# Ten tiles in one 51-token buffer: a weighted pair sum with rooms of 13, 13, 13 and 12 tokens, a GpSimd share in one tile, and the last three stores on SyncE

## The chip, the core and the metric

The kernel runs on one core of a Trainium2 chip. The core has a memory of 128 partitions (SBUF), and engines that work side by side: VectorE (DVE in the profile), ScalarE (ACT), GpSimd (POOL) and SyncE (SP), which here only issues transfers. Data come from and go to the main memory (HBM) by DMA: an engine's queue issues a transfer, and 16 DMA engines carry it out. The metric is the time of one execution in microseconds of the device (us); lower is better. The profile's span runs from the first to the last instruction and is a little shorter than this time.

## What is computed

```python
batch, seq, hidden, n_experts, k = 16, 1024, 512, 8, 2
# expert_outputs: (batch, seq, k, hidden) float32;  combine_weights: (batch, seq, k) float32
weights = combine_weights[..., np.newaxis]
out = np.sum(expert_outputs * weights, axis=2).astype(np.float32)
```

For each of 16,384 tokens, two vectors of 512 numbers are multiplied by a weight each and added. 64 MiB are read and 32 MiB are written.

## The kernel before

Each partition holds 128 tokens ("rows" in what follows): a row is one token in each of the 128 partitions, 4 KB per partition to read and 2 KB to write. The first 120 rows are laid out so that partition p has 120 neighbouring tokens, 480 KB; the last 8 rows are a second block of the same kind. The tiles are 12 rows, ten times, and then one of 8. Four buffers take turns, so a load of tile g waits until the store of tile g - 4 has landed.

```python
    per = n // P                     # 128 rows
    J, LAST = 12, 8
    main = per - LAST                # 120
    def rows(x):
        a = x[0 : P * main, :].rearrange("(p t) f -> p t f", p=P)
        b = x[P * main : n, :].rearrange("(p t) f -> p t f", p=P)
        return lambda t, c: a[:, t : t + c, :] if t < main else b[:, t - main : t - main + c, :]
    # ... (types; eo, cw and o are inputs and output seen through rows)
    last = main // J                 # 10
    ipool = ctx.enter_context(tc.tile_pool(name="in", bufs=4))
    # ... (weights wt: two small loads from ScalarE's queue; one activation to load its table)
    for g in range(last + 1):
        et = ipool.tile([P, J, k * h], dt)
        ot = et.rearrange("p j f -> p (j f)")[:, 0 : J * h].rearrange("p (j f) -> p j f", f=h)
        t0, c = g * J, J if g < last else LAST
        for a, m in ((0, 2), (2, c - 2)) if g == 0 else ((0, c),):
            nc.sync.dma_start(out=et[:, a : a + m], in_=eo(t0 + a, m), max_dma_last_dim=...)   # loads
        if g < last - 1:
            # wb: the tile's weights, each broadcast over 512 numbers; ek: et as 2 c vectors
            nc.vector.tensor_tensor(out=ek, in0=ek, in1=wb, op=mult)
            nc.vector.tensor_tensor(out=ot, in0=et[:, :, 0:h], in1=et[:, :, h : 2 * h], op=add)
            nc.scalar.dma_start(out=o(t0, c), in_=ot)                    # stores, ScalarE's queue
            continue
        for i in range(c):           # the last two tiles
            t = t0 + i
            nc.scalar.activation(out=et[:, i, 0:h], in_=et[:, i, 0:h], func=copy, scale=wt[:, 2*t : 2*t+1])
            if g == last:            # last tile: row by row, behind ScalarE
                nc.vector.scalar_tensor_tensor(out=ot[:, i, :], in0=et[:, i, h : 2 * h],
                    scalar=wt[:, 2*t+1 : 2*t+2], in1=et[:, i, 0:h], op0=mult, op1=add)
        if g < last:                 # last but one: VectorE multiplies the second vectors, then adds
            # w1: second weight of each row, broadcast; x1 = et[:, :, h : 2 * h]
            nc.vector.tensor_tensor(out=x1, in0=x1, in1=w1.to_broadcast([P, c, h]), op=mult)
            nc.vector.tensor_tensor(out=ot, in0=et[:, :, 0:h], in1=x1, op=add)
        nc.sync.dma_start(out=o(t0, c), in_=ot[:, 0:c])                  # last two stores, SyncE's queue
```

The sums are written over the tile's own first half, and stored from there. The order in which a queue issues is set by the scheduler that turns this text into a program, not by the text alone.

Of the kernel before, what the change touches and what calls it, by code (L numbers as in the profile page):

```python
# [1 line left out]

# [4 lines left out]


@with_exitstack
def kernel(  # L10
    ctx: ExitStack,
    tc: tile.TileContext,
    expert_outputs: bass.AP,
    combine_weights: bass.AP,
    out: bass.AP,
):

    nc = tc.nc  # L20
    b, s, k, h = expert_outputs.shape
    assert k == 2
    n = b * s
    P = nc.NUM_PARTITIONS
    per = n // P
    assert per * P == n
    J, LAST = 12, 8
    main = per - LAST
    assert main % J == 0
    eo = expert_outputs.rearrange("b s k h -> (b s) (k h)")  # L30
    cw = combine_weights.rearrange("b s k -> (b s) k")
    o = out.rearrange("b s h -> (b s) h")
# [7 lines that stand above are left out]
    eo, cw, o = rows(eo), rows(cw), rows(o)  # L40

    dt = mybir.dt.float32
    mult = mybir.AluOpType.mult
    add = mybir.AluOpType.add
    copy = mybir.ActivationFunctionType.Copy

    last = main // J

    wpool = ctx.enter_context(tc.tile_pool(name="w", bufs=1))
    ipool = ctx.enter_context(tc.tile_pool(name="in", bufs=4))  # L50

    wt = wpool.tile([P, per * k], dt)

    for t, c in ((0, main), (main, LAST)):
        nc.scalar.dma_start(
            out=wt[:, k * t : k * (t + c)].rearrange("p (t k) -> p t k", k=k), in_=cw(t, c)
        )

    warm = wpool.tile([P, 1], dt)
    nc.scalar.activation(out=warm, in_=nc.const_aps.tensor(1.0, (P, 1), dt), func=copy)  # L60

    for g in range(last + 1):
        et = ipool.tile([P, J, k * h], dt)

        ot = et.rearrange("p j f -> p (j f)")[:, 0 : J * h].rearrange("p (j f) -> p j f", f=h)
        t0, c = g * J, J if g < last else LAST

        for a, m in ((0, 2), (2, c - 2)) if g == 0 else ((0, c),):
            nc.sync.dma_start(  # L69
                out=et[:, a : a + m],  # L70
                in_=eo(t0 + a, m),
                max_dma_last_dim=k * h * 4 if g + a == 0 else None,
            )
        if g < last - 1:

            wb = wt[:, g * J * k : (g + 1) * J * k].unsqueeze(2).to_broadcast([P, J * k, h])
            ek = et.rearrange("p j (k h) -> p (j k) h", k=k)
            nc.vector.tensor_tensor(out=ek, in0=ek, in1=wb, op=mult)  # L78
            nc.vector.tensor_tensor(out=ot, in0=et[:, :, 0:h], in1=et[:, :, h : 2 * h], op=add)  # L79
            nc.scalar.dma_start(out=o(t0, c), in_=ot)  # L80
            continue


        for i in range(c):
            t = t0 + i
            nc.scalar.activation(  # L86
                out=et[:, i, 0:h], in_=et[:, i, 0:h], func=copy, scale=wt[:, 2 * t : 2 * t + 1]
            )
            if g == last:
                nc.vector.scalar_tensor_tensor(  # L90
                    out=ot[:, i, :],
                    in0=et[:, i, h : 2 * h],
                    scalar=wt[:, 2 * t + 1 : 2 * t + 2],
                    in1=et[:, i, 0:h],
                    op0=mult,
                    op1=add,
                )
        if g < last:
            w1 = wt.rearrange("p (t k) -> p t k", k=k)[:, t0 : t0 + c, 1:2]
            x1 = et[:, :, h : 2 * h]  # L100
            nc.vector.tensor_tensor(out=x1, in0=x1, in1=w1.to_broadcast([P, c, h]), op=mult)  # L101
            nc.vector.tensor_tensor(out=ot, in0=et[:, :, 0:h], in1=x1, op=add)  # L102
        nc.sync.dma_start(out=o(t0, c), in_=ot[:, 0:c])


# [1 line left out]
_INS = ['expert_outputs', 'combine_weights']  # L107
_OUTS = [((16, 1024, 512), 'float32')]


# [23 lines left out]
```

## Time and profile before

| | |
|---|---|
| time, median of 3 runs | 239.04 us (238.97 to 239.12) |
| span in the profile | 237.3 us |
| VectorE busy | 193.9 us (82%), 28 instructions |
| ScalarE busy | 14.0 us (6%), 22 instructions |
| GpSimd busy | 0.2 us (four fills at the start) |
| HBM read / written | 67.24 MB / 33.55 MB, 425 GB/s over the span |
| load of 12 rows, issue to landing, median | 29.9 us |
| store of 12 rows from ScalarE's queue, issue to landing, median | 32.7 us |

In the profile's groups a line reads: line of the kernel, engine, operation, output and inputs with their shapes, count; then total busy us and mean ns of one; then the engine's idle time before these instructions and what ended it. Lines 78 and 79 are the multiply and the add of an ordinary tile, 86 the ScalarE multiply of the last two tiles, 90 the row-by-row operation of the last tile, 101 and 102 the multiply and add of the last but one. Line 69 issues loads, 80 the stores from ScalarE, 103 those from SyncE. A "q" after an engine's name is its queue of DMA issues.

### The profile page before, as it was taken

The numbers are of one execution on the slowest core, as the hardware profiler recorded it, in microseconds if no ns is written. First come the engines' busy times: TensorE is split into PE (matmuls) and PEld (weight loads), VectorE is DVE, ScalarE is ACT, GpSimd is POOL, SyncE is SP. The second block draws the span as 40 slices with busy tenths as digits, with TensorE's granted clock in tenths as the row PEclk, the third lists the DMA queues.
The fourth block names the chain that finished last, engine by engine and source line by source line (L and its number), as shares of the span: only waits on it lengthen the run. The fifth ranks groups of instructions, "written<-read, shape, count | busy, mean of one in ns | idle before, by whom it ended". The sixth has DMA issues, their size and how long they took to land.

```text
span 237.3 us, 154 instructions
## 1 busy us (share of the span) xinstructions
DVE 193.9 (82%) x28; ACT 14.0 (6%) x22; POOL 0.2 (0%) x4
## 2 busy tenths in 40 slices
DVE  0008999999999999999999879969996998785710
ACT  2000000000000000000000000000000000740800
POOL 0000000000000000000000000000000000000000
DMA  8999999989899999999897999999997979999997
GB/s 308 443 456 406 398 431 497 398 356 505 356 439 435 427 464 464 398 398 522 348 522 344 452 427 435 464 464 398 398 522 340 530 336 460 458 403 442 402 438 309
DMA packets 3728, 100.80 MB, mean 425 GB/s; under 512 B 528, under 2 KB 656, under 8 KB 912
## 3 DMA queue, kind: packets, MB, share of 16 engines
q1 hardware_dynamic: 2144, 72.35, 71.1%
q10 hardware_dynamic: 1584, 28.44, 27.9%
HBM read 67.24 MB, written 33.55 MB: 425 GB/s over the span
## 4 chain that ended last, share of the span: by engine, by line
DMA 59%; DVE 33%; ACT 2%; DVEq 0%; ACTq 0%; issue 0%; SPq 0%
DMA et<-in_expert_outputs_dram 30%; DMA out_dram<-et 29%; DVE et L78 22%; DVE et L79 11%; ACT et L86 2%; DVE et L90 1%; DVEq L129 0%; ACTq L129 0%; SPq L69 0%; DVEq L78 0%; ACTq L86 0%
## 5 line engine op out<-in xcount | busy, mean ns | idle before, releaser
L78 DVE TENSOR_TENSOR et<-et,wt 128x12288 f32<-128x12288 f32 x9 | 116.6, 12955 | 25.2 <-DMA et<-in_expert_outputs_dram 25.2
L79 DVE TENSOR_TENSOR et<-et 128x6144 f32<-128x6144 f32 x9 | 59.0, 6558 | 0.3
L86 ACT ACTIVATE et<-et,wt 128x512 f32<-128x512 f32 x20 | 12.5, 707 | 209.2 <-DMA et<-in_expert_outputs_dram 209.2
L90 DVE SCALAR_TENSOR_TENSOR et<-et,wt 128x512 f32<-128x512 f32 x8 | 5.6, 748 | 3.9 <-ACT et L86 3.7
L101 DVE TENSOR_TENSOR et<-et,wt 128x6144 f32<-128x6144 f32 x1 | 6.6, 6559 | 2.3 <-DMA et<-in_expert_outputs_dram 2.3
L102 DVE TENSOR_TENSOR et<-et 128x6144 f32<-128x6144 f32 x1 | 6.6, 6559 | 0.9 <-ACT et L86 0.9
L60 ACT ACT_TABLE_LOAD x1 | 1.3, 1283 | 1.7 <-issue 1.7
L60 ACT ACTIVATE warm<-const-float32-1.0 128x1 f32<-128x1 f32 x1 | 0.2, 202 | 0.0
L118 POOL MEMSET const-bfloat16-1.0<- 128x1 bf16 x1 | 0.1, 102 | 0.0
L118 POOL MEMSET const-uint8-127<- 128x1 uint8 x1 | 0.1, 102 | 0.0
L118 POOL MEMSET const-float32-0.0<- 128x1 f32 x1 | 0.1, 99 | 0.2 <-issue 0.2
L118 POOL MEMSET const-float32-1.0<- 128x1 f32 x1 | 0.1, 99 | 0.0
## 6 DMA issues: line engine op xcount, KB each, us to landing
et<-in_expert_outputs_dram SPq DMA_DIRECT2D x9, 6144.0 KB, 29.9
out_dram<-et ACTq DMA_DIRECT2D x9, 3072.0 KB, 32.7
et<-in_expert_outputs_dram SPq DMA_DIRECT2D x1, 5120.0 KB, 17.3
et<-in_expert_outputs_dram SPq DMA_DIRECT2D x1, 4096.0 KB, 25.1
out_dram<-et SPq DMA_DIRECT2D x1, 3072.0 KB, 14.6
out_dram<-et SPq DMA_DIRECT2D x1, 2048.0 KB, 10.0
et<-in_expert_outputs_dram SPq DMA_DIRECT2D x1, 1024.0 KB, 5.4
wt<-in_combine_weights_dram ACTq DMA_DIRECT2D x1, 120.0 KB, 4.4
```

The source lines that it names most:

```text
L60: nc.scalar.activation(out=warm, in_=nc.const_aps.tensor(1.0, (P, 1), dt), func=copy)
L78: nc.vector.tensor_tensor(out=ek, in0=ek, in1=wb, op=mult)
L79: nc.vector.tensor_tensor(out=ot, in0=et[:, :, 0:h], in1=et[:, :, h : 2 * h], op=add)
L86: nc.scalar.activation(out=et[:, i, 0:h], in_=et[:, i, 0:h], func=copy, scale=wt[:, 2 * t : 2 * t + 1])
L90: nc.vector.scalar_tensor_tensor(out=ot[:, i, :], in0=et[:, i, h : 2 * h], scalar=wt[:, 2 * t + 1 : 2 * t + 2], in1=et[:, i, 0:h], op0=mul ...
L101: nc.vector.tensor_tensor(out=x1, in0=x1, in1=w1.to_broadcast([P, c, h]), op=mult)
L102: nc.vector.tensor_tensor(out=ot, in0=et[:, :, 0:h], in1=x1, op=add)
L118: nc = _bacc.Bacc("TRN2", target_bir_lowering=False, num_devices=1)
```

## The change

The tiles become 13, 13, 13, 12 rows, twice, and then two of 13: ten in all. They lie in four "rooms" of one buffer of 51 rows, where before there were four buffers of 12. The first block is now 115 rows (460 KB per partition), the second 13. Fewer and larger tiles use the SBUF that was left over. In the last tile but one, ScalarE multiplies the first vectors of seven rows and GpSimd those of the other six, while VectorE multiplies the second vectors; for this tile VectorE reads its weights from a copy in PSUM, a separate memory of the core, so that it has one input in SBUF and can run beside GpSimd. The stores of the last three tiles go out from SyncE's queue, behind the last loads, where before it was the last two.

```diff
-    J, LAST = 12, 8
+    rooms = [13, 13, 13, 12]
+    sizes = rooms * 2 + [13, 13]
+    LAST = sizes[-1]
     main = per - LAST
...
-    ipool = ctx.enter_context(tc.tile_pool(name="in", bufs=4))
+    ipool = ctx.enter_context(tc.tile_pool(name="in", bufs=1))
+    ppool = ctx.enter_context(tc.tile_pool(name="pw", bufs=1, space=bass.MemoryType.PSUM))
...
-    for g in range(last + 1):
-        et = ipool.tile([P, J, k * h], dt)
+    pw = ppool.tile([P, sizes[-2] * k], dt)
+    nc.vector.tensor_copy(out=pw, in_=wt[:, k * (main - sizes[-2]) : k * main])
+    room = ipool.tile([P, sum(rooms), k * h], dt)
+    t0 = 0
+    for g, c in enumerate(sizes):
+        at = sum(rooms[: g % len(rooms)])
+        et = room[:, at : at + c]
...
-            nc.scalar.dma_start(out=o(t0, c), in_=ot)
-            continue
-        for i in range(c):
+        else:
+            m = c if g == last else 7
+            for i in range(m):
                 # ScalarE's multiply; in the last tile VectorE's row operation behind it, as before
...
-        if g < last:
-            w1 = wt.rearrange("p (t k) -> p t k", k=k)[:, t0 : t0 + c, 1:2]
+            if g < last:
+                w0 = wt.rearrange("p (t k) -> p t k", k=k)[:, t0 + m : t0 + c, 0:1]
+                w1 = pw.rearrange("p (t k) -> p t k", k=k)[:, :, 1:2]
+                x0, x1 = et[:, m:c, 0:h], et[:, :, h : 2 * h]
+                nc.gpsimd.tensor_tensor(
+                    out=x0, in0=x0, in1=w0.to_broadcast([P, c - m, h]), op=mult
+                )
                 # VectorE's multiply of x1 by w1 and its add, as before
...
-        nc.sync.dma_start(out=o(t0, c), in_=ot[:, 0:c])
+        queue = nc.scalar if g < last - 2 else nc.sync
+        queue.dma_start(out=o(t0, c), in_=ot)
+        t0 += c
```

More of the change, by code (lines that the diff above doesn't have):

```diff
@@ L26 @@
     assert per * P == n
-    J, LAST = 12, 8
+    rooms = [13, 13, 13, 12]
+    sizes = rooms * 2 + [13, 13]
+    assert sum(sizes) == per
+    LAST = sizes[-1]
     main = per - LAST
-    assert main % J == 0
     eo = expert_outputs.rearrange("b s k h -> (b s) (k h)")
@@ L45 @@
     copy = mybir.ActivationFunctionType.Copy
-    last = main // J
+    last = len(sizes) - 1
     wpool = ctx.enter_context(tc.tile_pool(name="w", bufs=1))
-    ipool = ctx.enter_context(tc.tile_pool(name="in", bufs=4))
+    ipool = ctx.enter_context(tc.tile_pool(name="in", bufs=1))
+    ppool = ctx.enter_context(tc.tile_pool(name="pw", bufs=1, space=bass.MemoryType.PSUM))
     wt = wpool.tile([P, per * k], dt)
@@ L60 @@
     nc.scalar.activation(out=warm, in_=nc.const_aps.tensor(1.0, (P, 1), dt), func=copy)
-    for g in range(last + 1):
-        et = ipool.tile([P, J, k * h], dt)
-        ot = et.rearrange("p j f -> p (j f)")[:, 0 : J * h].rearrange("p (j f) -> p j f", f=h)
-        t0, c = g * J, J if g < last else LAST
+    pw = ppool.tile([P, sizes[-2] * k], dt)
[5 more added lines that the diff above has]
+        et = room[:, at : at + c]
+        ek = et.rearrange("p j (k h) -> p (j k) h", k=k)
+        ot = ek[:, 0:c]
         for a, m in ((0, 2), (2, c - 2)) if g == 0 else ((0, c),):
@@ L74 @@
         if g < last - 1:
-            wb = wt[:, g * J * k : (g + 1) * J * k].unsqueeze(2).to_broadcast([P, J * k, h])
-            ek = et.rearrange("p j (k h) -> p (j k) h", k=k)
+            wb = wt[:, t0 * k : (t0 + c) * k].unsqueeze(2).to_broadcast([P, c * k, h])
             nc.vector.tensor_tensor(out=ek, in0=ek, in1=wb, op=mult)
             nc.vector.tensor_tensor(out=ot, in0=et[:, :, 0:h], in1=et[:, :, h : 2 * h], op=add)
-            nc.scalar.dma_start(out=o(t0, c), in_=ot)
-            continue
@@ L84 @@
-        for i in range(c):
[L85 to L96, printed above, removed]
-                )
@@ L98 @@
-        if g < last:
-            w1 = wt.rearrange("p (t k) -> p t k", k=k)[:, t0 : t0 + c, 1:2]
-            x1 = et[:, :, h : 2 * h]
-            nc.vector.tensor_tensor(out=x1, in0=x1, in1=w1.to_broadcast([P, c, h]), op=mult)
-            nc.vector.tensor_tensor(out=ot, in0=et[:, :, 0:h], in1=x1, op=add)
-        nc.sync.dma_start(out=o(t0, c), in_=ot[:, 0:c])
+        else:
+            m = c if g == last else 7
+            for i in range(m):
+                t = t0 + i
+                nc.scalar.activation(
+                    out=et[:, i, 0:h], in_=et[:, i, 0:h], func=copy, scale=wt[:, 2 * t : 2 * t + 1]
+                )
+                if g == last:
+                    nc.vector.scalar_tensor_tensor(
+                        out=ot[:, i, :],
+                        in0=et[:, i, h : 2 * h],
+                        scalar=wt[:, 2 * t + 1 : 2 * t + 2],
+                        in1=et[:, i, 0:h],
+                        op0=mult,
+                        op1=add,
+                    )
[5 more added lines that the diff above has]
+                    out=x0, in0=x0, in1=w0.to_broadcast([P, c - m, h]), op=mult
+                )
+                nc.vector.tensor_tensor(out=x1, in0=x1, in1=w1.to_broadcast([P, c, h]), op=mult)
+                nc.vector.tensor_tensor(out=ot, in0=et[:, :, 0:h], in1=x1, op=add)
```

## The prediction

> **What bounds the kernel now.** I read the page's DMA parts first, because the arithmetic is small against the bytes: 67.24 MB are read and 33.55 MB written. Then I asked for the busy time in stretches, the waits, the groups, and the timeline of the end.
>
> ```profile
> DMA  8999999989899999999897999999997979999997
> ...
> q1 hardware_dynamic: 2144, 72.35, 71.1%
> q10 hardware_dynamic: 1584, 28.44, 27.9%
> ```
>
> The last column is packet time as a share of 16 engines' span. 71.1 + 27.9 = 99.0% of 237.3 us is 234.9 us per DMA engine, so 2.4 us of the span hold no transfer. The stretches show where (columns: stretch, length, busy of VectorE, ScalarE and GpSimd, clock, DMA share, GB/s; a packet counts where it starts):
>
> ```profile
> 0.00:2.00 2.00, 0.00 (x0) 0.26 (x1) 0.20 (x4) 1.00 0.20 31
> 2.00:20.00 18.00, 1.36 (x1) 1.22 (x2) 0.00 (x0) 1.00 1.06 441
> 20.00:60.00 40.00, 39.93 (x5) 0.00 (x0) 0.00 (x0) 1.00 0.99 423
> 60.00:120.00 60.00, 59.90 (x7) 0.00 (x0) 0.00 (x0) 1.00 1.00 433
> 120.00:180.00 60.00, 54.50 (x6) 0.00 (x0) 0.00 (x0) 1.00 1.00 433
> 180.00:220.00 40.00, 32.63 (x4) 7.53 (x13) 0.00 (x0) 1.00 1.00 430
> 220.00:236.00 16.00, 5.57 (x8) 4.94 (x8) 0.00 (x0) 1.00 0.99 424
> 236.00:237.30 1.30, 0.00 (x0) 0.00 (x0) 0.00 (x0) 1.00 0.00 0
> ```
>
> From 2 to 236 us the DMA share is 0.99 to 1.06: the transfers never pause, not even while the last tile is computed. The idle 2.4 us are the start (first packet near 1.8 us) and the final wait. VectorE is at 82% and waits for data:
>
> ```profile
> DVE et L78 <- DMA et<-in_expert_outputs_dram: 25.2, 4, 18.6
> ...
> SPq L69 <- DMA out_dram<-et: 173.8, 7, 45.5
> ```
>
> 18.6 of the 25.2 us are the first load; the other three waits are 2.2 us each, one per tile late in the run. SyncE's 173.8 us are loads waiting for a store to free their buffer; with other transfers always pending, that wait costs nothing. At 433 GB/s a row (one token of each of the 128 partitions) costs 0.524 MB / 433 = 1.21 us to load and 0.605 us to store, 1.815 us together. Twelve rows make 21.8 us, and the late VectorE tiles start at 137.66, 159.43 and 181.13, which is 21.7 us apart. So **the bound is the bytes**, from end to end.
>
> **What the skill says.** "DMA: Bandwidth & Descriptors", section "Where 436 GB/s comes from", gives 16 ports a ceiling of 435.2 GB/s; the 433 here agrees, so nothing is left in the rate. Its section "Queues, rings and completion order" says that SyncE and ScalarE each own a queue on the same 16 engines, consumed in order, and that an engine alternates between queues packet by packet. Here a load's packet is 48 KB and a store's 24 KB, so two busy queues share 2:1; a 6,144 KB load needs 12 x 1.21 = 14.5 us alone and landed after a median 29.9 us, which fits the sharing. "SBUF — State Buffer", section "SBUF: two separate sides", says VectorE with two SBUF inputs and GpSimd lock each other out of a shared port pair; this is why the change puts one tile's weights into PSUM. No run so far shows it. "GPSIMD Engine Reference", section 3.1, has 4,497 ns for a two-input fp32 operation of 2,048 elements; I use it below.
>
> **Part 1: ten tiles instead of eleven.** Bytes stay. One load and one store go. Queue q10 has 1,584 packets for 11 DMAs, so 144 each: 128 of data and 16 of completion, or 8 + 1 per engine. By the packet records a 49,152-byte packet takes 1.815 us and a 24,576-byte one 0.912, so the fixed part is 2 x 0.912 - 1.815 = 0.009 us. Two DMAs x 9 packets x 0.009 = **0.16 us saved**. The first load grows a row, so VectorE begins 1.2 us later, at about 19.8; the second load is already queued behind it, and DMA loses nothing.
>
> **Part 2: VectorE's work.**
>
> ```profile
> L78 DVE TENSOR_TENSOR et<-et,wt 128x12288 f32<-128x12288 f32 x9 | 116.6, 12955 | 25.2 <-DMA et<-in_expert_outputs_dram 25.2
> L79 DVE TENSOR_TENSOR et<-et 128x6144 f32<-128x6144 f32 x9 | 59.0, 6558 | 0.3
> L86 ACT ACTIVATE et<-et,wt 128x512 f32<-128x512 f32 x20 | 12.5, 707 | 209.2 <-DMA et<-in_expert_outputs_dram 209.2
> L90 DVE SCALAR_TENSOR_TENSOR et<-et,wt 128x512 f32<-128x512 f32 x8 | 5.6, 748 | 3.9 <-ACT et L86 3.7
> ```
>
> A row of an ordinary tile costs (12.955 + 6.558) / 12 = 1.626 us. Eight such tiles hold 102 rows: 165.9 us. The last but one costs 13/12 x 6.56 = 7.1 us for the multiply and 7.1 for the add, 14.2. The last took 5.78 us for 8 rows, so 13 take 9.4. The sum is 189.5 against 193.9. A tile of 13 needs 21.1 us of VectorE and 13 x 1.815 = 23.6 of DMA: the bound stays with DMA, and VectorE's 4.4 us are worth nothing. The copy of 26 weights to PSUM falls between their landing (about 5 us) and the first tile.
>
> **Part 3: GpSimd.** Six rows are 3,072 elements; from the skill's figure an estimate of 3,072/2,048 x 4.5 = 6.7 us. ScalarE's seven rows cost 7 x 0.707 = 4.9, VectorE's multiply beside them 7.1. All three end near 7.2 us after the load, against 7.5 now for 12 rows (202.96 to 210.46).
>
> **Part 4: the end.** The last load is now 13 rows instead of 8, with 3.6 us more VectorE work between it and the last store. Is DMA kept busy? Count back from the last byte, at 235.9. Three stores are queued behind the last load on SyncE: 12, 13 and 13 rows, 7.3 + 7.9 + 7.9 = 23.1 us. So the last load's bytes end at 235.9 - 23.1 = 212.8. It lands 0.8 us later; VectorE runs from 214.3 (one ScalarE row first) to 223.7. The last store is needed at 235.9 - 7.9 = 228.0, and reaches the engines 1.1 us after issue (the first load: 0.73 to 1.8), so VectorE may end at 226.8: **3.1 us of slack**. The last store but one is needed at 220.1, so its add must end by 219.0. Its load ends before the last load's 15.7 us, by 197.1; with 0.8 and 7.2 + 7.1 that is 212.2, or 6.8 us of slack. GpSimd could take twice its estimate. So the longer tail is covered, because 7.3 + 7.9 us of stores wait behind the last load. Sum: 239.04 - 0.16 = **238.9 us**.
>
> **Rivals.** (a) *SyncE's order puts a store before the last load.* The source asks for tile 7's store before the loads of tiles 8 and 9, and SyncE waits in order. For: that store comes early in the text. Against: the queue is reordered by when things are ready. Before, tile 9's store also stands ahead of load 10, yet the load went out at 194.8 and the store at 217.0. Load 9 needs tile 5's store landed: VectorE has done six tiles (77 rows) at 19.8 + 77 x 1.626 = 145, and the median store, 32.7 us for 12 rows, is 35.4 for 13, so about 180. The store of tile 7 needs its add: 19.8 + 165.9 = 185.7 and two waits of some 2 us, about 190. That is 10 us of margin instead of 22. If it happened for load 9, that load's end would move 7.3 us later, 4.2 beyond the slack: 243.2 us. For load 8 too, some 10 us more: about 253. I give this 7%.
> (b) *The longer tail shows.* If GpSimd and VectorE blocked each other through the whole tile, 6.7 us would come on top of 14.3; that still fits the 6.8 us. Only past this does each further microsecond count: 240 to 242. About 5%.
> (c) *The transfers get cheaper.* A 460 KB pitch instead of 480 KB could suit memory better. The 20 to 60 us stretch ran at 423 GB/s: 40 x 10/433 = 0.9 us below the later rate. Some of that might come back: 238.0. Nothing in the profile offers more.
> (d) *VectorE becomes the bound.* At 21.1 against 23.6 us a tile this has no support.
>
> **Range and chances.** The 234.9 us of packet time stay under any arrangement, so 2% faster (234.3) would need a faster transfer rate: 1%. Slower by 2% (243.8) needs rival (a) in its worse form: 4%. Range 238.2 to 240.0; below it stands (c) in full, above it (a) and (b).
>
> **What would show it.** Right: DMA share near 1.00 in every stretch up to 1.5 us from the end; VectorE waits of about 2.5 us for late loads; SyncE issuing both last loads ahead of the three stores; last landing near 213.6; VectorE done near 224. Wrong: a stretch after 200 us with a DMA share under 0.9, a store between the last loads on SyncE, an add of the last tile but one ending after 219, or a steady rate that is not 433 GB/s.

## The result, and the profile after

The kernel after takes 239.74 us (median of 6 runs, 239.40 to 240.45) against 239.04 for the kernel before: a ratio of 1.0031, with a 95% interval of 1.0016 to 1.0045. Beside the last experiments it was timed again: 240.08 us (12 runs, 239.93 to 240.49), ratio 1.0032 (1.0016 to 1.0048). By these ratios the change costs about 0.75 us, a small loss but clear of noise, where a gain of 0.16 was predicted. The ratio is not simply the quotient of the two medians: the runs of the kernel before spread to 240.9 us, as the table below shows, and the medians alone differ by 0.70 and 1.04 us.

The DMA queues of the kernel after (queue and kind; packets, MB, share of 16 engines' span):

```profile
q1 hardware_dynamic: 2144, 77.07, 75.3%
q10 hardware_dynamic: 1296, 23.72, 23.1%
```

98.4% of 238.7 us is 234.9 us of packet time per DMA engine, as before, although 288 packets are gone. The same stretches, with the last one longer by the growth of the span (columns as in the prediction; the GpSimd column is the third count):

```profile
20.00:60.00 40.00, 39.93 (x4) 0.00 (x0) 0.00 (x0) 1.00 1.00 421
60.00:120.00 60.00, 59.90 (x7) 0.00 (x0) 0.00 (x0) 1.00 1.00 433
120.00:180.00 60.00, 54.39 (x6) 0.00 (x0) 0.00 (x0) 1.00 1.00 434
180.00:220.00 40.00, 29.51 (x11) 9.53 (x16) 5.32 (x1) 1.00 1.00 431
220.00:236.00 16.00, 4.72 (x8) 2.95 (x5) 0.00 (x0) 1.00 0.99 426
236.00:238.70 2.70, 0.00 (x0) 0.00 (x0) 0.00 (x0) 1.00 0.05 20
```

The transfers still never pause, and the steady rate is still 433. The 421 GB/s from 20 to 60 us, for 423 before, is no clear sign: in e12, the same kernel once more, that stretch has 423 again. What differs is the end. After 236 us, where the kernel before started no packet, a few still start, and so they do in e12:

```profile
236.00:238.30 2.30, 0.00 (x0) 0.00 (x0) 0.00 (x0) 1.00 0.06 23
```

A share of 0.05 over all 16 engines is one or two engines that finish late.

The end, in order of time (start, duration, engine, line, operation):

```profile
184.16 0.33 SPq L80 DMA_DIRECT2D room<-in_expert_outputs_dram  x1
...
191.22 33.85 SPq L118 DMA_DIRECT2D out_dram<-room  x3
195.16 4.40 ACT L96 ACTIVATE room<-room,wt 128x512 f32<-128x512 f32 x7 [191.92 <-DMA room<-in_expert_outputs_dram]
195.16 7.09 DVE L115 TENSOR_TENSOR room<-room,pw 128x6656 f32<-128x6656 f32 x1 [3.96 <-DMA room<-in_expert_outputs_dram]
195.36 5.32 POOL L112 TENSOR_TENSOR room<-room,wt 128x3072 f32<-128x3072 f32 x1 [194.92 <-DMA room<-in_expert_outputs_dram]
202.38 7.09 DVE L116 TENSOR_TENSOR room<-room 128x6656 f32<-128x6656 f32 x1
214.87 8.07 ACT L96 ACTIVATE room<-room,wt 128x512 f32<-128x512 f32 x13 [15.31 <-DMA room<-in_expert_outputs_dram]
215.63 9.09 DVE L100 SCALAR_TENSOR_TENSOR room<-room,wt 128x512 f32<-128x512 f32 x13 [6.16 <-ACT room L96]
```

SyncE issued the last load at 184.16, ahead of the three stores. GpSimd ran beside VectorE's multiply, which took 7.09 us, as long as in e3 without GpSimd. VectorE ended at 224.7. So the tail works as described, and the loss must be elsewhere.

**Where the time went.** Dividing the DMA share by the rate, short windows show how long a packet took. Around the first store the kernel before shows

```profile
38.00:40.00 2.00, 2.00 (x2) 0.00 (x0) 0.00 (x0) 1.00 0.93 393
40.00:42.00 2.00, 2.00 (x1) 0.00 (x0) 0.00 (x0) 1.00 1.16 393
```

and the kernel after

```profile
42.00:44.00 2.00, 2.00 (x1) 0.00 (x0) 0.00 (x0) 1.00 0.99 426
44.00:46.00 2.00, 2.00 (x1) 0.00 (x0) 0.00 (x0) 1.00 1.21 426
46.00:48.00 2.00, 2.00 (x1) 0.00 (x0) 0.00 (x0) 1.00 1.54 586
```

In each pair the same bytes start in 2 us, but their packets take 25% (before) and 22% (after) longer in the second window. In the third, 1.54 / 586 is 13% over 0.99 / 426. The records of single packets say it exactly. The first store is issued at 38 us (before) and 41 us (after). Some 3 us later each engine starts a load packet that stands next to its first store packet, and this load takes 0.3 to 0.6 us longer than normal (1.815 us for 48 KB, 1.966 for 52 KB). The records don't name the engine, but each large packet starts where another has just ended, to within a few ns, so that they can be joined into 16 chains. Before, there is about one such packet per engine. After, 14 engines have two, while the other two have one packet each that is 1.19 and 1.44 us too long. Once this turn from loads alone to loads and stores is over, packets take their normal time to the end. The Trainium skill's "DMA: Bandwidth & Descriptors", section "The descriptor swizzle", has each engine serve its own set of partitions in a transfer over all 128. The records agree in number: the 128 packets of the last store of e8 and of e11, which start after a pause, come in eight rounds of 16. So an engine that falls behind stays behind (the trace after is of the longest of its six runs): before, all end by 236.17; after, 14 end by 236.3 and those two at 237.05 and 237.46. In all but one of the profiles made here, the time is the last engine's last byte plus 2.9 to 3.1 us (after 237.46 and 240.45, before 236.17 and 239.08).

### The profile page after: what moved, and what is told of

Its sections match the earlier page's. It is cut to its first block, busy times and chain, and to the rows that moved or that the text cites. A ratio compares the mean times of both kernels' runs of the same rounds, so it can differ in the third digit from the quotient of the medians.

```text
span 238.7 us, 162 instructions
## 1 busy us (share of the span) xinstructions
DVE 188.7 (79%) x32; ACT 14.0 (6%) x22; POOL 5.5 (2%) x5
## 4 chain that ended last, share of the span: by engine, by line
DMA 63%; DVE 28%; ACT 2%; issue 0%; DVEq 0%; ACTq 0%; SPq 0%
DMA room<-in_expert_outputs_dram 35%; DMA out_dram<-room 28%; DVE room L88 18%; DVE room L89 9%; DVE room L100 2%; ACT room L96 2%; DVEq L144 0%; ACTq L144 0%; SPq L80 0%; DVEq L88 0%; ACTq L96 0%
## 5 line engine op out<-in xcount | busy, mean ns | idle before, releaser
L88 DVE TENSOR_TENSOR room<-room,wt 128x13312 f32<-128x13312 f32 (+1 forms) x8 | 110.0, 13756 | 19.8 <-DMA room<-in_expert_outputs_dram 19.8
L89 DVE TENSOR_TENSOR room<-room 128x6656 f32<-128x6656 f32 (+1 forms) x8 | 55.7, 6958 | 0.3
L96 ACT ACTIVATE room<-room,wt 128x512 f32<-128x512 f32 x20 | 12.5, 710 | 207.2 <-DMA room<-in_expert_outputs_dram 207.2
L100 DVE SCALAR_TENSOR_TENSOR room<-room,wt 128x512 f32<-128x512 f32 x13 | 8.9, 748 | 6.4 <-ACT room L96 6.2
L115 DVE TENSOR_TENSOR room<-room,pw 128x6656 f32<-128x6656 f32 x1 | 7.1, 7086 | 4.0 <-DMA room<-in_expert_outputs_dram 4.0
L112 POOL TENSOR_TENSOR room<-room,wt 128x3072 f32<-128x3072 f32 x1 | 5.3, 5320 | 194.9 <-DMA room<-in_expert_outputs_dram 194.9
L116 DVE TENSOR_TENSOR room<-room 128x6656 f32<-128x6656 f32 x1 | 7.1, 7092 | 0.1
```

What stands on the lines that cost most here:

```text
L112: nc.gpsimd.tensor_tensor(out=x0, in0=x0, in1=w0.to_broadcast([P, c - m, h]), op=mult)
```

## The experiments

All were compared with the kernel before on the same chip. "Long packets" is the sum of time over the normal from 35 to 65 us, as a mean per DMA engine, and "last byte" is when the slowest engine ended; both are from the packet records of the one run that was traced.

| run | tiles, first block | median us (range, runs) | ratio (95%) | long packets | last byte |
|---|---|---|---|---|---|
| before | 12, 480 KB | 239.04 to 239.13 in four groups (238.94-240.89) | 1 | 0.60 | 236.17 |
| after | 13, 460 KB | 239.74 (239.40-240.45, 6) | 1.0031 (1.0016-1.0045) | 0.86 | 237.46 |
| e1 | 12, 460 KB, one tile in two pieces | 240.90 (239.41-241.15, 10) | 1.0063 (1.0045-1.0081) | 0.44 | 236.39 |
| e2 | 13, 480 KB | 239.88 (239.49-240.53, 21) | 1.0024 (1.0011-1.0036) | 1.10 | 236.87 |
| e3 | 13, 460 KB | 240.32 (239.99-241.11, 9) | 1.0042 (1.0024-1.0060) | 1.04 | 237.20 |
| e4 | 13, 460 KB | 240.13 (239.61-240.33, 11) | 1.0037 (1.0025-1.0050) | 0.92 | 237.32 |
| e5 | 12, 480 KB | 239.98 (239.07-241.05, 16) | 1.0013 (0.9993-1.0033) | 0.71 | 237.06 |
| e6 | 13, 460 KB | 239.93 (239.59-240.45, 22) | 1.0019 (1.0006-1.0031) | 0.74 | 237.01 |
| e7 | first 12, 460 KB | 261.57 (260.16-262.30, 6) | 1.0921 (1.0884-1.0957) | 0.38 | 257.14 |
| e8 | 13, 460 KB | 244.34 (244.02-246.05, 4) | 1.0223 (1.0185-1.0262) | 1.02 | 240.93 |
| e9 | 13, one queue | 242.46 (242.15-242.57, 4) | 1.0133 (1.0107-1.0160) | 0.74 | 239.44 |
| e10 | 12, one queue | 243.34 (243.08-243.89, 4) | 1.0175 (1.0146-1.0204) | 1.43 | 240.88 |
| e11 | 13, 460 KB | 247.49 (246.98-247.56, 4) | 1.0346 (1.0315-1.0378) | 0.90 | 243.97 |
| e12 | after again | 240.08 (239.93-240.49, 12) | 1.0032 (1.0016-1.0048) | 1.01 | 237.09 |

The spread matters. The kernel before and e5 have runs down to 238.9 and 239.07, and others up to 240.9 and 241.05. No run of any kernel with 13-row tiles was below 239.40.

With two queues the long packets follow the first large store, not the layout: 0.86 to 1.10 us where it has 13 rows (after, e2, e3, e4, e8, e11, e12), 0.38 to 0.74 where it has 12 (before, e1, e5, e6, e7). The second group includes 460 KB layouts (e1, e6, e7), and in e7 loads of 13 rows beside that store. It is one trace of each kernel, and the time does not follow this mean: e1 has few long packets in its trace, and a long time.

The late engines can be followed further. A load packet over 1.1 us too long stands right behind its engine's first store packet, and that engine began to store about 2 us before the rest: two engines in the trace after (44.75 and 45.07, the others from 46.58), three in e4, one in e5 (41.70, the others from 43.37), four in e12. In each of these four traces as many engines end late, 0.5 us or more behind the rest. In e3 five begin early and five end late. In the kernel before all 16 begin within 43.26 to 43.78, and none ends late. So late engines go with a first store that begins in two groups. They need not: in e2 nine begin early and seven later, and the ends are even. What decides it was not tested.

**e1, the layout alone.** From the kernel before:

```diff
-    main = per - LAST
+    main = 115
+    def parts(t, c):
+        return ((t, c),) if t >= main or t + c <= main else ((t, main - t), (main, t + c - main))
# loads and SyncE's stores go over parts(t0, c)
```

> The kernel before (tiles of 12, last 8) with the first block cut to 115 rows, 460 KB per partition; the tile that crosses the boundary is loaded and stored in two pieces, two transfers more (0.16 us). Theory S, layout: the loss comes from DMA engines that are stalled for unequal times when the first stores meet the loads, and the layout in memory sets how unequal: 239.6 to 240.1, some engines over 0.5 us later than the rest at the end, runs spread by over 0.5 us. Theory S, tile size: the same stalls, but set by the 13-row packets: 239.1 to 239.3 with the spread of before. Theory G (GpSimd, PSUM and the rest of the new program cost a fixed time): 239.1 to 239.3.

240.90 us: time is lost without larger tiles, and more than the theory had. The edit also cuts a tile in two pieces, and no run separates that from the layout, so that the layout is the cause is not shown. And the profiled run was one of only two in ten near 239.4, and it has few long packets. So the trace doesn't show what the other eight runs lost; that stays open.

**e2, the large tiles alone.** From the kernel after:

```diff
-    sizes = rooms * 2 + [13, 13]
+    sizes = rooms * 2 + [9, 9, 8]
-            m = c if g == last else 7
+            m = c if g == last else 5
```

> The kernel after, but tiles of 13, 13, 13, 12 twice and then 9, 9, 8, so that the first block has 120 rows and 480 KB per partition as before; GpSimd has four of the nine rows of the last tile but one. As many transfers as before. Layout: 239.0 to 239.2, engines ending together. Tile size: 239.5 to 239.9, stragglers. Fixed cost of GpSimd and PSUM: 239.6 to 239.8.

239.88 us, with the most long packets of the two-queue runs (1.10 us per engine). Time is lost without the new layout. e2 also holds the rest of the change. Against e5 below, which has that rest with 12-row tiles, its median is no longer (239.98), but none of its 21 runs is below 239.49, where seven of e5's 16 are at 239.25 or less: with 13-row tiles the shortest times are gone. Here no engine is far behind: the 16 engines end evenly from 236.2 to 236.9, where those of the kernel before end from 235.7 to 236.2.

**e3, without GpSimd and PSUM.** From the kernel after:

```diff
-            m = c if g == last else 7
+            m = c
-                w1 = pw.rearrange("p (t k) -> p t k", k=k)[:, :, 1:2]
+                w1 = wt.rearrange("p (t k) -> p t k", k=k)[:, t0 : t0 + c, 1:2]
# pw, its copy and the GpSimd multiply are gone
```

> The kernel after without GpSimd and without the weights in PSUM: ScalarE multiplies all 13 rows of the last tile but one. Stalled engines: 239.7, as after, because that tile has slack. Fixed cost of GpSimd and PSUM: 238.9 to 239.1.

240.32 us: no time comes back, so GpSimd and PSUM are not the cost. The add begins 8.1 us after the load's landing instead of 7.2, inside the slack.

**e4, an early write.** From the kernel after:

```diff
     nc.scalar.activation(out=warm, in_=nc.const_aps.tensor(1.0, (P, 1), dt), func=copy)
+    nc.scalar.dma_start(out=o(0, 1)[:, :, 0:1], in_=warm.unsqueeze(2))
```

> The kernel after with one small store at about 3 us: 4 bytes to the first output row of every partition, overwritten later by the first real store. If the stalls at 44 to 48 us are the price of the first write to each partition's stretch of the output, they go or move to about 4 us, and the time is 239.0 to 239.4. If they come from reads and writes meeting, whatever was written before, the long packets at 44 to 48 us stay and the time is 239.7.

240.13 us, and 29 of 30 clearly long load packets (by over 0.1 us) still lie from 44 to 48 us. So an earlier write of 4 bytes to each partition's stretch of the output does not take them away.

**e5, the rest of the change alone.** From the kernel after:

```diff
-    rooms = [13, 13, 13, 12]
-    sizes = rooms * 2 + [13, 13]
+    rooms = [12, 12, 12, 12]
+    sizes = rooms * 2 + [12, 12, 8]
```

> Everything of the change but its sizes: tiles of 12 (last 8) in four rooms of one buffer, 480 KB per partition, GpSimd with five rows of the last tile but one, weights in PSUM, last three stores on SyncE. Theory: the loss lies in DMA engines that stall when the first store begins, more with 13-row packets; then this is the kernel before in time, 239.0 to 239.2, with a mean stall near 40 us of about 0.6 us per engine. Rival: the three stores on one queue or GpSimd cost time at the end; then 239.5 to 239.9, with a pause of the transfers after 200 us.

By its interval e5 can't be told from the kernel before, and seven of its 16 runs are between 239.07 and 239.25. The other nine are at 239.96 and above, so its median misses the expectation. The profiled run was one of these (240.04), and it looks like the kernel after: the transfers don't pause, 15 engines end by 236.22 and one at 237.06, and one load packet at 42.6 us is 1.17 us too long. The seven runs, within 0.3 us of the usual 239.0 of the kernel before, leave no room for a larger fixed cost of the tail and GpSimd, and the straggler (the one late engine) turns out to be a matter of chance that 12-row tiles meet too.

**e6, a soft start.** From the kernel after:

```diff
-        queue.dma_start(out=o(t0, c), in_=ot)
+        for a, m in ((0, 1), (1, c - 1)) if g == 0 else ((0, c),):
+            queue.dma_start(out=o(t0 + a, m), in_=ot[:, a : a + m])
```

> The kernel after with the first tile's store in two transfers, one row (2 KB packets) and then twelve. If the stall comes from all 16 engines beginning to write large packets at once, small first packets shrink it: long load packets near 44 us mostly gone, 239.0 to 239.4. If any start of writing beside loads stalls the loads, the long packets stay: 239.7 to 240.0.

239.93 us, but the trace tells more than the time. In e6's short windows:

```profile
44.00:46.00 2.00, 2.00 (x1) 0.00 (x0) 0.00 (x0) 1.00 1.02 440
...
58.00:60.00 2.00, 2.00 (x1) 0.00 (x0) 0.00 (x0) 1.00 0.97 369
60.00:62.00 2.00, 2.00 (x2) 0.00 (x0) 0.00 (x0) 1.00 1.53 565
```

At 44 us, where the kernel after has 1.21 share for 426 GB/s, the packets are normal although stores have begun: they are the 2 KB ones, one to each load packet, from 44.2 to 57.9 us by the records. The long load packets come at 58 to 62, with the first *large* store packets, which start at 60.1. So in this trace the loads are stretched where large writes begin, and not where small ones do. The small packets didn't avoid it; it came some 14 us later.

**e7, a first store of 12 rows.** From the kernel after:

```diff
-    rooms = [13, 13, 13, 12]
+    rooms = [12, 13, 13, 13]
-        queue = nc.scalar if g < last - 2 else nc.sync
+        queue = nc.scalar if g < last else nc.sync
```

> The kernel after with rooms of 12, 13, 13, 13, so that the first store has packets of 24 KB as before, and begins at about 38 us, beside loads with packets of 52 KB; only the last store is on SyncE, which should cost nothing since transfers stay pending. If the size of the first store's packets or its moment sets the stall: 239.0 to 239.3. If the size of the loads' packets does: 239.6 to 240.1.

261.57 us (260.16 to 262.30, 6 runs, ratio 1.0921, interval 1.0884 to 1.0957), for a reason that the edit brought with it: the last tile but one has 13 rows and now begins in a room of 12, so it reaches into the room of the last tile. In e7's timeline the last load therefore waits until tile 8 is added:

```profile
204.37 7.09 DVE L116 TENSOR_TENSOR room<-room 128x6656 f32<-128x6656 f32 x1
211.49 0.33 SPq L80 DMA_DIRECT2D room<-in_expert_outputs_dram  x1
...
238.34 8.07 ACT L96 ACTIVATE room<-room,wt 128x512 f32<-128x512 f32 x13 [36.84 <-DMA room<-in_expert_outputs_dram]
```

So the time can't settle whether the first store's size matters. The packet records speak for it: beside this first store of 12 rows, seven load packets are over 0.2 us too long, none over 0.52, and the sum is 0.38 us per engine, although the loads there have 52 KB. They also show the turn a second time. When the last load begins after a pause, together with tile 8's store, 15 of its first 16 packets are 1.0 to 1.7 us too long, near 212.5 us. The run shows besides that one shared row of 51 costs some 22 us, and that the order of the room sizes isn't free.

**e8, the order of rival (a).** From the kernel after:

```diff
+        if g == last:
+            nc.vector.tensor_copy(out=et[:, 0, 0:1], in_=ot7[:, 11, 0:1])   # ot7: tile 7's sums
         for a, m in ((0, 2), (2, c - 2)) if g == 0 else ((0, c),):
```

> The kernel after with SyncE's order forced: a copy of one element, from the last row of tile 7's sums to the first element of the last tile's room, makes the last load wait until tile 7 is added, so that its store is issued first. The prediction's rival (a) says that the last load then ends 7.3 us later, which is 4.2 us over the slack: 243 to 244, with about 4 us of idle DMA just before the last store. If the tail has more slack than was counted: 240 to 241.

244.34 us (244.02 to 246.05, 4 runs, ratio 1.0223, interval 1.0185 to 1.0262). In e8's timeline:

```profile
201.88 0.33 SPq L82 DMA_DIRECT2D room<-in_expert_outputs_dram  x1
...
222.12 8.07 ACT L98 ACTIVATE room<-room,wt 128x512 f32<-128x512 f32 x13 [23.01 <-DMA room<-in_expert_outputs_dram]
```

and its stretches:

```profile
225.00:230.00 5.00, 5.00 (x9) 5.00 (x9) 0.00 (x0) 1.00 0.66 282
230.00:235.00 5.00, 1.96 (x3) 0.18 (x1) 0.00 (x0) 1.00 0.60 256
```

The last load lands at 222.1 instead of 214.8, 7.3 us later, which is the time of the store put before it; no pause comes before it, although the copy lets it go only at 201.88. From 225 to 235 us the transfers are idle for 5 x 0.34 + 5 x 0.40 = 3.7 us.

**e9 and e10, one queue.** From the kernel after; e10 has also e5's sizes:

```diff
+    for g in range(3):
+        load(g)                       # the loads, as a function
     for g, c in enumerate(sizes):
...
-        queue = nc.scalar if g < last - 2 else nc.sync
+        queue = nc.sync
         queue.dma_start(out=o(t0, c), in_=ot)
+        if g + 3 <= last:
+            load(g + 3)
```

> The kernel after with every store on SyncE's queue too, three tiles loaded ahead: load 0, 1, 2, store 0, load 3, store 1, load 4 and so on. Loads and stores follow each other on each DMA engine and never alternate; VectorE's 21.1 us a tile against 23.6 of DMA leave something pending at all times. If the stalls near 44 us come from the first large store packets alternating with load packets, they go: all engines end together, 238.2 to 238.9, with small spread. If any first large write stalls the loads near it, long packets remain at the first store and the time is 239.3 to 240. If one queue alone carries less: 241 or more, with a rate under 433 GB/s.

> The same on one queue with tiles of 12 (last 8), 480 KB per partition. Alternation theory: 238.4 to 239.0, without the second cluster near 240 that the kernel before sometimes shows. Any first large write: as before, 239.0 with some runs near 240.

242.46 and 243.34 us. The alternation theory falls. In e9's stretches:

```profile
46.00:48.00 2.00, 2.00 (x1) 0.00 (x0) 0.00 (x0) 1.00 0.99 426
48.00:50.00 2.00, 2.00 (x1) 0.00 (x0) 0.00 (x0) 1.00 1.33 426
...
180.00:220.00 40.00, 24.82 (x7) 7.52 (x13) 5.32 (x1) 1.00 0.98 422
...
236.00:237.00 1.00, 0.00 (x0) 0.00 (x0) 0.00 (x0) 1.00 0.31 133
237.00:238.00 1.00, 0.00 (x0) 0.00 (x0) 0.00 (x0) 1.00 0.31 133
238.00:239.00 1.00, 0.00 (x0) 0.00 (x0) 0.00 (x0) 1.00 0.25 106
```

All 16 engines have a long load packet at the first turn from loads to a store, without alternation. Later in e9 the records show two to nine clearly long load packets at each store (near 71, 84, 95, 120, 143, 166, 190 and 213 us): 1.02 us per engine after 65 us, where two queues have 0.01 to 0.07 (but 1.48 in e7 and 0.33 in e8, whose last load waits). Nothing evens this out, and from 236 to 239 us only about a quarter to a third of the engines work. In these traces two queues that alternate pay once, and one queue in order pays at each turn. e9 and e10 also fix how far loads run ahead (three tiles), which no run separates from the order.

**e11, a longer tail.** From the kernel after:

```diff
-        if g < last - 1:
+        if g != last - 1:
```

> The kernel after with the last tile wholly on VectorE (multiply of 26 vectors, add of 13, no ScalarE), so that it takes 21.1 us after the last landing instead of 9.9. If the tail's slack is the 2.6 us that the trace after leaves (3.1 were predicted), the time grows by 11.2 - 2.6 = 8.6: 248 to 249. If the last store never waits for DMA, by 11: 251. If much more is hidden: under 246.

247.49 us (246.98 to 247.56, 4 runs, ratio 1.0346, interval 1.0315 to 1.0378), a little under the expectation. In e11's stretches:

```profile
220.00:225.00 5.00, 5.00 (x1) 0.00 (x0) 0.00 (x0) 1.00 0.99 426
225.00:230.00 5.00, 4.97 (x2) 0.00 (x0) 0.00 (x0) 1.00 0.59 256
230.00:235.00 5.00, 5.00 (x1) 0.00 (x0) 0.00 (x0) 1.00 0.00 0
235.00:240.00 5.00, 0.02 (x1) 0.00 (x0) 0.00 (x0) 1.00 0.99 421
```

The queued stores last until about 228, as counted; then DMA waits for VectorE, which ends at 235.0. After that pause all 16 engines end within 0.2 us of each other (243.8 to 244.0), so that what stragglers lost before it is not seen at the end. That may be why it costs 7.4 us more than e12 (240.08) and not 8.6; it was not tested.

**e12, the kernel after again**, unchanged, beside e9 to e11:

> The kernel after once more, beside the others on one chip: 239.4 to 240.4, with no run below 239.3, and DMA engines that end up to 1 us apart because of long packets near 44 us.

240.08 us with no run below 239.93, and 29 clearly long load packets between 42 and 48 us: as expected, and the loss repeats.

## Why the prediction held in range and missed the sign

- **The bound**, held: from 2 to 236 us the DMA share is 0.99 to 1.03 in every stretch, and the steady rate 433 GB/s.
- **Part 1**, half right. The normal packet time fell from 233.55 to 233.41 us per engine, 0.14 for 0.16 predicted. The step that failed is the last one, "239.04 - 0.16": it takes every packet at its normal time and lets the end follow the mean of the engines. Near the first store long packets rose by 0.26 us per engine (0.41 in e12), more than the 0.14. Even so, all packets together take 234.83 us per engine before and 234.92 after, nearly the same mean. But the last two engines end about 1 us after the others, at 237.05 and 237.46, where all ended by 236.17 before. The time is set by the last engine, not by the mean that the page's share gives. "DMA loses nothing" was said of the start, where it holds; the first store was not looked at. And "under any arrangement" was too much for the 234.9 us: e10 has 236.94.
- **The range** was luck: its upper part stood for rivals (a) and (b), which didn't occur, and 239.74 lies in it for a reason that it did not have. The 240.08 of e12 lies just above it.
- **Rival (c)** looked at the right place, the 20 to 60 us stretch below 433, with the wrong sign: the lost time there was taken for something to win, and the long packets grew from 0.60 to 0.86 us per engine (1.01 in e12).
- **Part 2**, right: 188.7 us of VectorE for 189.5, worth nothing.
- **Part 3**, right in the mechanism, its estimate too high: GpSimd took 5.32 us, not 6.7; the add began 7.2 us after the landing, as counted. That VectorE isn't locked out with its weights in PSUM agrees with this trace: its multiply took 7.09 us beside GpSimd, and 7.09 in e3 without it. No run had GpSimd beside such a multiply with both inputs in SBUF, so what the copy in PSUM is worth isn't shown.
- **Part 4**, right within 1.2 us: last landing 214.8 for 213.6, VectorE done 224.7 for 223.7, so 2.1 us of slack for 3.1 by the same count. (The last byte before, counted from as 235.9, was at 236.17 by the records, so each deadline lies 0.3 later.) e11 puts the end of the queued stores near the 228.0 counted.
- **Rival (a)** didn't occur, with 7 us of margin for the 10 counted (the last load was issued at 184.16, tile 7's store at 191.22), but is real: e8 measures 244.34 for 243.2.
- **Rivals (b) and (d)** didn't occur: the add of the last tile but one ended at 209.5, well before 219, and VectorE never became the bound.

Which part set off the loss is only partly settled. Kernels with the larger tiles (e2) and with the new layout (e1) each lose time against the kernel before, though neither edit is alone in its run; the losses don't add up, and the rest of the change can't be told from nothing (e5). That late engines set the end is shown by their last bytes; that 13-row stores make them likelier is argued from the traces. Why packets should be stretched twice, and what happens in memory at the turn, was not shown.

## What to carry to other kernels

When the transfers never pause, look at when each DMA engine ends and not at their mean: work is dealt out in fixed shares, so one late packet early in the run is still there at the end. A longer tail is free as long as stores of its length are queued behind the last load; count back from the last byte and check it against the issue order. And where loads and stores kept one core's DMA full, two queues that alternate did better than one in order, in both cases tried.

## What was not expected of the hardware

- Where large stores begin beside loads, load packets took 0.2 to 1.7 us longer than their normal 1.8 to 2.0; beside 2 KB stores they didn't (e6), and an earlier small write doesn't prevent it (e4).
- One queue in order was slower than two that alternate: e9 by 1.0% against e12, e10 by 1.75% against the kernel before and 1.4% against e5, with the same tiles and no pause of the transfers before the end.
- GpSimd multiplied 128 x 3,072 numbers by broadcast weights in 5.32 us, 1.73 ns each per partition, where ScalarE needs about 0.62 us for 512 (8.07 us for 13 rows).
